# Half-width Fourier stages, with the mirrored half written in reverse, in a hybrid Fourier and attention backbone

## The chip, the cores and the metric

One core of one Trainium2 chip. The metric is the device time of one execution in microseconds. Before the change three runs took 1893.22 to 1894.74 us, median 1894.34.

## What is computed

Two layers over 256 latent tokens and 256 context tokens of width 1024. In each layer a projection feeds two mixers side by side, attention and a two-dimensional Fourier transform of 4 groups of 128 channels; their outputs are gated, merged, projected and added back, and a feed-forward part follows (dense in layer 0, eight experts with two per token in layer 1). The part that matters here:

```python
def fourier_mix(u):
    b, t, _ = u.shape
    ug = u.astype(jnp.float32).reshape(b, t, N_FOURIER_GROUPS, FOURIER_GROUP)
    f = jnp.fft.fft2(ug, axes=(1, 3), norm="ortho").real
    return f.reshape(b, t, FOURIER_WIDTH).astype(u.dtype)
```

Only the real part is kept. With A = u times the channel cosines, B = u times the channel sines, the result is cos(token) A - sin(token) B.

## The kernel before, in words

Activations lie with channels on the 128 partitions and tokens along the free dimension. Weights stream in from HBM through the SP queue, 1 MB at a time; ACT copies each piece to a reduced float32 form (`wh`, L169) and DVE subtracts to get the remainder (`wl`, L181), and a product is taken as three matmuls (`mm3`, L212 to L214). Large activations are held the same way, as a high and a low part.

Within a mixer the order of the instructions is the order in which the Python program writes them. There are two background queues, attention and modulation. Every call of `tick()` gives each queue some credit, and when the credit reaches one, the next step of that queue is written into the program at that place. So pieces of attention (scores L494 to L499, maximum L501 and L503 on DVE, exponentials L512 and L513 on ACT, normalisation L520 to L522 on DVE, transposes L534 on PE, their high part L535 on ACT and low part L536 on DVE, values L546 and `half` L551, L554) stand between the products of the projections, and modulation (L318, L320 on DVE) as well. Each engine then works through its own instructions strictly in that order.

The Fourier part works by group g of 128 channels and by stream s of 256 tokens. Layer 0 has two streams, latent and context; layer 1 has the latent one alone. That makes 8 streams in layer 0 and 4 in layer 1.

- `fourier_first` (L589): for each half of 128 tokens, one float32 matmul of U against `four_c`, 256 columns: 128 cosines, then 128 sines. The two halves share a PSUM tile `psab`; one ACT copy (L598) brings its 512 columns to SBUF as `ab`.
- `fourier_second` (L603): four float32 matmuls of 256 columns (L607, L608) add up the cosine and the sine part over both token halves in one PSUM tile `psf`; ACT copies it to the high part of `ft` (L611), DVE subtracts to get the low part (L612).
- `mixer` (L902) calls them: `first(0)`, the projection of U for group 2, then for g = 0, 1, 2 in layer 0 `second(g)`, `first(g + 1)`, in layer 1 the other way about, and at last `second(3)`. Right behind it `halves(ft)` multiplies all four chunks of `ft` with the weights.

`psab`, `psf` and the projection tiles `psp` share the PSUM tag "mm" with three buffers. The SBUF tag "rr" with two buffers holds the rotary temporaries and `half` of the attention.

Of the kernel before, what the change touches and what calls it, by code (L numbers as in the profile page):

```python
# [11 lines left out]
F32 = mybir.dt.float32  # L12
F32R = mybir.dt.float32r
I32 = mybir.dt.int32
AF = mybir.ActivationFunctionType
OP = mybir.AluOpType
# [5 lines left out]
TL = 256  # L22
# [53 lines left out]
def hybrid_kernel(ctx, tc, x, c, ctx_in, c_ctx, w_mod, b_mod, norm1_g, norm2_g, w_in, sink, w_fourier,  # L76
# [3 lines left out]
    V, A, P_, G, S = nc.vector, nc.scalar, nc.tensor, nc.gpsimd, nc.sync  # L80
# [29 lines left out]
    def tick(n=1):  # L110
        for _ in range(n):
            ticks[0] += 1
            for q in ("attn", "mod"):
                credit[q] += pace[q]
                if credit[q] >= 1.0:
                    credit[q] -= 1.0
                    step(q)
# [470 lines left out]

    def fourier_first(streams, sb, ps_pool, u, nab):  # L589

        r = []
        for s in range(streams):
            ps = ps_pool.tile([128, 2, 256], F32, name="psab", tag="mm", bufs=3)
            for k in range(2):
                t0 = s * 256 + k * 128
                P_.matmul(ps[:, k, :], u[:, t0:t0 + 128], four_c, start=True, stop=True)
            ab = sb.tile([128, 2, 256], F32, name="ab", tag="ab", bufs=nab)
            A.activation(ab, ps, AF.Copy)  # L598
            r.append(ab)
            tick()  # L600
        return r

    def fourier_second(abs_, g, ps_pool, f_out):  # L603
        for s, ab in enumerate(abs_):
            ps = ps_pool.tile([128, 512], F32, name="psf", tag="mm", bufs=3)[:, :256]
            for k in range(2):
                P_.matmul(ps, ab[:, k, 0:128], four_t(0, k), start=(k == 0), stop=False)  # L607
                P_.matmul(ps, ab[:, k, 128:256], four_t(1, k), start=False, stop=(k == 1))  # L608
                tick()
            sl = slice(s * 256, (s + 1) * 256)  # L610
            A.activation(f_out[:, 0, g, sl], ps, AF.Copy)  # L611
            V.tensor_tensor(f_out[:, 1, g, sl], ps, f_out[:, 0, g, sl].bitcast(F32), op=OP.subtract)  # L612

    def mixer_units(l):
        base = l * D * IN_W
# [34 lines left out]
    four_c = tabp.tile([128, 256], F32, name="four_c")  # L650
# [11 lines left out]
    four_t = lambda a, k: tab[1 + a][:, k * 256:(k + 1) * 256]  # L662
# [13 lines left out]
    psA = psA_st.enter_context(tc.tile_pool(name="psA", bufs=2, space=PSUM))  # L676
# [225 lines left out]
    def mixer(l, limbs, r16, psk, psv, when_mixed=None, when_merging=None, pre=(), xp=None, room=None):  # L902
        n = T2 if l == 0 else TL
# [11 lines left out]
        at = attn_st.enter_context(tc.tile_pool(name=f"attn{l}", bufs=1))  # L915
# [33 lines left out]
        U, AB = {}, {}  # L949
# [30 lines left out]
        ft = r16.tile([128, 2, 4, n], F32R, name="ft", tag="ro")  # L980
        o = r16.tile([128, 2, 4, n], F32R, name="o", tag="ro")
# [4 lines left out]
            AB[g] = fourier_first(n // 256, lp, psA, U.pop(g), 2)  # L986

        def second(g):
            fourier_second(AB.pop(g), g, psA, ft)

        def late_q(j):
            while prog["scores"] < 2 * (j - 1) * (n // 128):
# [37 lines left out]
        for p in range(2):  # L1030
            for i, ps in halves(ft):
                f = 4 * p + i
                pool, tag, bufs = ((lp, "U", 2), (lp, "ab", 2), (tabp, "tab", 3), (lp, "q1", 1))[
                    2 * p + (i % 2 if p == 0 else i == 3)]
# [8 lines left out]
            for i in range(4):  # L1043
                f = 4 * p + i
                t = gate(lp, "q0", 1)
# [18 lines left out]
        for p in range(2):  # L1064
            th = early_th[4 * p:4 * p + 4] or [gate(mg, "th", 4) for _ in range(4)]
            for i, ps in halves(o):
                f = 4 * p + i
                y = th[i][:, :n]
                V.scalar_tensor_tensor(y, y, 1.0, ps[:, :n], op0=OP.add, op1=OP.mult)
                if owed:  # L1070
# [4 lines left out]
                                                             op=OP.subtract))  # L1075
# [53 lines left out]
    with ExitStack() as st:  # L1129
# [44 lines left out]
        for a, b in PARTS:  # L1174
            ah = r16.tile([128, 8, T2], F32R, name="ah", tag="ro")
            al = r16.tile([128, 8, T2], F32R, name="al", tag="ro")
            for j in range(a, b, 2):
                sg = []
                for br in range(2):
                    for k in range(2):  # L1180
                        if j == 0 and br == 0:
                            ps = first[k]
                        else:
                            wh, wl = stream.take()
                            ps = psA.tile([128, 512], F32, name="psp", tag="mm", bufs=3)
                            mm3(stream, ps, wh, wl, range(8), [(hh[:, i, :], hl[:, i, :]) for i in range(8)])
                        if br == 0:
                            t = ff.tile([128, 512], F32, name="sg", tag="sg", bufs=3)
                            A.activation(t, ps, AF.Silu)
                            sg.append(t)  # L1190
                        else:
                            i = j - a + k
                            t = ff.tile([128, 512], F32, name="af", tag="af", bufs=2)
# [823 lines left out]
```

## Time and profile before

| | before |
|---|---|
| median of 3 runs, us | 1894.34 |
| profiled execution, us | 1891.14 |
| its span, us | 1889.3 |
| mean granted TensorE clock | 0.991 |
| PE busy, us (share of the span) | 1805.1 (96%) |
| DVE busy, us | 1507.3 (80%) |
| ACT busy, us | 1131.6 (60%) |

The span runs from the first to the last recorded instruction; 1.84 us of the profiled execution lie around it. Busy time is the time in which an engine had at least one instruction at work. The busy times are means over stages with different limits, so windows and the order of instructions in time have to be read beside them. In the rows below, a number in square brackets behind an instruction is the engine's idle time before it, with the engine, tile and line that ended it. PE is the matmul, PEld its weight load.

### The profile page before, as it was taken

The page shows a single profiled execution, that of the slowest core. Times are in us where ns is not written, and L with a number is a line of the kernel's source. Part 1 is how long each engine was busy: PE and PEld are TensorE (multiplying, and loading weights), DVE is VectorE, ACT ScalarE, POOL GpSimd, SP SyncE. Part 2 cuts the span into 40 slices and gives each one's busy share as a digit, 9 for nine tenths or more (in the row PEclk, how much of TensorE's full clock was granted, in tenths as well). Part 3 has the DMA queues.
Part 4 walks back from the last instruction along what each step waited for, and adds up shares of the span by engine and source line. Part 5 has one row for each costly group of instructions (what it writes and reads, how often), then busy time and mean ns, then how long its engine had stood idle before and what let it go on. Part 6 is the DMA issues. An engine that isn't in the chain of part 4 may idle for free. (4 is left out here: it accounts for less than half of the span.)

```text
span 1889.3 us, 27557 instructions
## 1 busy us (share of the span) xinstructions
PE 1805.1 (96%) x9701; PEld 1497.7 (79%) x9701; DVE 1507.3 (80%) x1772; ACT 1131.6 (60%) x1280; POOL 64.2 (3%) x95
## 2 busy tenths in 40 slices
PE   7999999999999999999999999999999999999996
PEld 4788877877777788899877878778887788888874
DVE  6787896577777436787788988999889988888897
ACT  5564622423122223665497877887778887787785
POOL 3200000200000001100000000000000000000000
PEclk9999999999999999999999999999999999999999
DMA  9313462265577223434898999999999999999992
GB/s 295 105 57 101 129 206 91 92 214 196 176 232 261 92 79 100 135 112 157 312 367 321 403 367 363 408 402 408 344 342 408 401 391 333 326 363 371 378 402 104
DMA packets 222530, 488.59 MB, mean 259 GB/s; under 512 B 11410, under 2 KB 106898, under 8 KB 222356
## 3 DMA queue, kind: packets, MB, share of 16 engines
q1 hardware_dynamic: 221076, 482.11, 70.6%
q0 software_dynamic: 1280, 4.20, 0.8%
q8 instruction: 105, 1.72, 0.4%
q14 instruction: 69, 0.57, 0.1%
HBM read 485.22 MB, written 1.05 MB: 257 GB/s over the span
## 5 line engine op out<-in xcount | busy, mean ns | idle before, releaser
L1373 DVE TENSOR_TENSOR el<-raw,eh 128x2048 fp32r<-128x2048 f32 (+2 forms) x333 | 727.7, 2211 | 92.1 <-PE pgt L1830 34.2
L1350 ACT ACTIVATE eh<-raw 128x2048 fp32r<-128x2048 f32 (+2 forms) x333 | 609.6, 1859 | 94.7 <-PE pgt L1830 56.9
L212 PE MATMUL psp<-hh,wh 128*128 128x512 f32 (+1 forms) x704 | 260.1, 370 | 2.6 <-ACT U L954 1.8
L214 PE MATMUL psp<-hh,wl 128*128 128x512 f32 (+1 forms) x704 | 255.6, 363 | 4.9 <-DVE wl L181 4.9
L213 PE MATMUL psp<-hl,wh 128*128 128x512 f32 (+1 forms) x704 | 254.5, 362 | 0.0
L181 DVE TENSOR_TENSOR wl<-raw,wh 128x1024 fp32r<-128x1024 f32 (+1 forms) x152 | 182.4, 1207 | 41.8 <-PE psp L214 20.8
L169 ACT ACTIVATE wh<-raw 128x1024 fp32r<-128x1024 f32 (+1 forms) x152 | 156.3, 1039 | 62.1 <-DMA raw<-in_w_down_d 24.9
L212 PEld LDWEIGHTS psp<-hh,wh 128*128 128x128 f32 x704 | 133.5, 190 | 31.1 <-issue 9.9
L214 PEld LDWEIGHTS psp<-hh,wl 128*128 128x128 f32 x704 | 133.2, 189 | 27.7 <-DVE wl L181 7.4
L213 PEld LDWEIGHTS psp<-hl,wh 128*128 128x128 f32 x704 | 133.5, 190 | 19.4 <-issue 0.5
L1830 PE MATMUL py<-el,eah 128*128 128x256 f32 (+1 forms) x712 | 126.1, 315 | 8.1 <-DVE el L1373 7.1
L1830 PEld LDWEIGHTS py<-el,eah 128*128 128x128 f32 x712 | 102.6, 190 | 35.8 <-DVE el L1373 27.5
L1830 PE MATMUL py<-eh,eah 128*128 128x512 f32 x440 | 121.2, 397 | 0.0
L320 DVE SCALAR_TENSOR_TENSOR acc<-rawm,cvec,acc 128x512 f32<-128x512 f32 x140 | 99.8, 748 | 1.4
L1830 PE MATMUL pup<-el,xh 128*128 128x256 f32 (+1 forms) x560 | 94.7, 307 | 4.4 <-DVE el L1373 4.3
L1830 PEld LDWEIGHTS pup<-el,xh 128*128 128x128 f32 x560 | 80.5, 188 | 20.1 <-DVE el L1373 11.9
L1830 PE MATMUL pgt<-el,xh 128*128 128x256 f32 (+1 forms) x480 | 84.6, 314 | 11.5 <-DVE el L1373 10.9
L1830 PE MATMUL pup<-eh,xh 128*128 128x512 f32 x336 | 93.9, 401 | 0.0
L1830 PEld LDWEIGHTS pgt<-el,xh 128*128 128x128 f32 x480 | 69.4, 189 | 28.5 <-DVE el L1373 20.7
L1830 PEld LDWEIGHTS py<-eh,eah 128*128 128x128 f32 x440 | 78.9, 189 | 14.6 <-ACT eh L1350 0.8
L1830 PE MATMUL pgt<-eh,xh 128*128 128x512 f32 x296 | 83.5, 404 | 0.7 <-ACT xh L1461 0.7
L1195 ACT ACTIVATE ah<-af 128x512 fp32r<-128x512 f32 x22 | 13.9, 632 | 99.7 <-DVE af L1194 99.7
(379 smaller groups left out, 3221.0 us busy)
## 6 DMA issues: line engine op xcount, KB each, us to landing
raw<-in_w_gate_e SPq DMA_DIRECT2D x112, 1024.0 KB, 7.8
raw<-in_w_down_e SPq DMA_DIRECT2D x110, 1024.0 KB, 7.7
raw<-in_w_up_e SPq DMA_DIRECT2D x109, 1024.0 KB, 8.0
rawm<-in_w_mod SPq DMA_DIRECT2D x112, 256.0 KB, 4.5
raw<-in_w_in SPq DMA_DIRECT2D x26, 1024.0 KB, 5.3
raw<-in_w_gate_d SPq DMA_DIRECT2D x11, 1024.0 KB, 5.5
raw<-in_w_up_d SPq DMA_DIRECT2D x11, 1024.0 KB, 5.5
mraw<-in_w_mod SPq DMA_DIRECT2D x16, 512.0 KB, 8.7
```

The source lines that it names most:

```text
L169: A.activation(h[:, :n, :], src, AF.Copy)
L181: self.eng.tensor_tensor(lo[:, :n, :], src, h[:, :n, :].bitcast(F32), op=OP.subtract)
L212: P_.matmul(ps, wh[:, k, :], ah, start=(start and i == 0), stop=False)
L213: P_.matmul(ps, wh[:, k, :], al, start=False, stop=False)
L214: P_.matmul(ps, wl[:, k, :], ah, start=False, stop=(stop and i == n - 1))
L320: V.scalar_tensor_tensor(acc[v], r, s, acc[v], op0=OP.mult, op1=OP.add)
L1195: A.activation(ah[:, i, :], t, AF.Copy)
L1350: A.activation(self.like(self.hi[i][:, sl], x), x, AF.Copy)
L1373: V.tensor_tensor(self.like(self.lo[i][:, sl], x), x, self.like(self.hi[i][:, sl], x).bitcast(F32), op=OP.subtract)
L1830: P_.matmul(ps[:, a:b], x[:, k, :], w[:, c + a:c + b], start=(start and ps_id[i] not in seen), stop=(stop and ps_id[i] not in ps_id[i + 1: ...
```

## The change

`fourier_first` multiplies the channel columns 0 to 64 of the cosines and of the sines alone, 130 columns in place of 256. `fourier_second` multiplies the token columns 0 to 128, 129 in place of 256, and keeps the cosine part (`even`) and the sine part (`odd`) in separate columns of the PSUM tile. The rest follows from cos(2 pi (n - j) k / n) = cos(2 pi j k / n) and the opposite sign for the sine: the missing half of `ab` is written backwards by two more ACT copies, one with scale -1, and the missing half of the result is even minus odd, written backwards by DVE. The sum and the difference form a new SBUF tile `f`, from which the high and the low part of `ft` are made. The temporaries `odd` and `f` take the tag "rr". The number of ticks stays the same.

```diff
     def fourier_first(streams, sb, ps_pool, u, nab):
-        r = []
+        r, h = [], 65
+        two = four_c.rearrange("p (a n) -> p a n", a=2)[:, :, 0:h]
+        turned = lambda t, a: bass.AP(tensor=t.tensor, offset=t.offset + a * 128 + 127,
+                                      ap=[list(t.ap[0]), [256, 2], [-1, 128 - h]])
         for s in range(streams):
-            ps = ps_pool.tile([128, 2, 256], F32, name="psab", tag="mm", bufs=3)
+            ps = ps_pool.tile([128, 2, 2, h], F32, name="psab", tag="mm", bufs=3)
             for k in range(2):
                 t0 = s * 256 + k * 128
-                P_.matmul(ps[:, k, :], u[:, t0:t0 + 128], four_c, start=True, stop=True)
+                P_.matmul(ps[:, k], u[:, t0:t0 + 128], two, start=True, stop=True)
             ab = sb.tile([128, 2, 256], F32, name="ab", tag="ab", bufs=nab)
-            A.activation(ab, ps, AF.Copy)
+            A.activation(ab.rearrange("p k (a n) -> p k a n", a=2)[:, :, :, 0:h], ps, AF.Copy)
+            A.activation(turned(ab, 0), ps[:, :, 0, 1:128 - h + 1], AF.Copy)
+            A.activation(turned(ab, 1), ps[:, :, 1, 1:128 - h + 1], AF.Copy, scale=-1.0)
             r.append(ab)
             tick()
         return r
 
-    def fourier_second(abs_, g, ps_pool, f_out):
+    def fourier_second(abs_, g, ps_pool, f_out, sb):
+        h = TL // 2 + 1
         for s, ab in enumerate(abs_):
-            ps = ps_pool.tile([128, 512], F32, name="psf", tag="mm", bufs=3)[:, :256]
-            for k in range(2):
-                P_.matmul(ps, ab[:, k, 0:128], four_t(0, k), start=(k == 0), stop=False)
-                P_.matmul(ps, ab[:, k, 128:256], four_t(1, k), start=False, stop=(k == 1))
+            ps = ps_pool.tile([128, 512], F32, name="psf", tag="mm", bufs=3)
+            even, odd = ps[:, 0:h], ps[:, 256:256 + h]
+            for i, p in enumerate((even, odd)):
+                for k in range(2):
+                    P_.matmul(p, ab[:, k, i * 128:(i + 1) * 128], four_t(i, k)[:, 0:h], start=(k == 0), stop=(k == 1))
                 tick()
+            o = sb.tile([128, 256], F32, name="odd", tag="rr", bufs=2)
+            f = sb.tile([128, 256], F32, name="f32", tag="rr", bufs=2)
+            A.activation(o[:, 0:h], odd, AF.Copy)
+            V.tensor_tensor(f[:, 0:h], even, o[:, 0:h], op=OP.add)
+            back_ = bass.AP(tensor=f.tensor, offset=f.offset + TL - 1, ap=[list(f.ap[0]), [-1, TL - h]])
+            V.tensor_tensor(back_, even[:, 1:TL - h + 1], o[:, 1:TL - h + 1], op=OP.subtract)
             sl = slice(s * 256, (s + 1) * 256)
-            A.activation(f_out[:, 0, g, sl], ps, AF.Copy)
-            V.tensor_tensor(f_out[:, 1, g, sl], ps, f_out[:, 0, g, sl].bitcast(F32), op=OP.subtract)
+            A.activation(f_out[:, 0, g, sl], f, AF.Copy)
+            V.tensor_tensor(f_out[:, 1, g, sl], f, f_out[:, 0, g, sl].bitcast(F32), op=OP.subtract)
```

In the changed kernel the two matmul lines are L600 and L617, ACT's copies L602, L603, L604 (`ab`), L621 (`odd`) and L626 (`ft`), and DVE's operations L622 (add), L624 (subtract) and L627 (low part of `ft`).

The order on DVE in layer 0, at `second(0)` (its two streams), before; `ft` is the Fourier result, `xlo` the low part of the attention weights, `st` and `p` its softmax:

```order
L503 TENSOR_SCALAR st<-st,sink_b 128x1
L612 TENSOR_TENSOR ft<-psf,ft 128x256
L536 TENSOR_TENSOR xlo<-ptr,xh 128x4x128
L520 TENSOR_TENSOR st<-st 128x1
L521 RECIPROCAL st<-st 128x1
L522 TENSOR_SCALAR p<-p,st 128x512
L612 TENSOR_TENSOR ft<-psf,ft 128x256
L501 TENSOR_REDUCE st<-pss 128x1
```

and in the changed kernel:

```order
L503 TENSOR_SCALAR st<-st,sink_b 128x1
L622 TENSOR_TENSOR f_924<-psf,odd 128x129
L624 TENSOR_TENSOR f_924<-psf,odd 128x127
L627 TENSOR_TENSOR ft<-f_924,ft 128x256
L536 TENSOR_TENSOR xlo<-ptr,xh 128x4x128
L520 TENSOR_TENSOR st<-st 128x1
L521 RECIPROCAL st<-st 128x1
L522 TENSOR_SCALAR p<-p,st 128x512
L622 TENSOR_TENSOR f_949<-psf,odd 128x129
L624 TENSOR_TENSOR f_949<-psf,odd 128x127
L627 TENSOR_TENSOR ft<-f_949,ft 128x256
L501 TENSOR_REDUCE st<-pss 128x1
```

Each place of L612 now holds three instructions in a row, and the attention steps between them stand where they stood.

The order on ACT at the same place, from the second stream of `second(0)` to the end of `first(1)`, before:

```order
L535 ACTIVATE xh<-ptr 128x4x128
L611 ACTIVATE ft<-psf 128x256
L598 ACTIVATE ab<-psab 128x512 x2
L512 ACTIVATE p,st<-pss,st 128x256
L513 ACTIVATE st<-sink_b,st 128x1
```

and in the changed kernel:

```order
L535 ACTIVATE xh<-ptr 128x4x128
L621 ACTIVATE odd<-psf 128x129
L626 ACTIVATE ft<-f_949 128x256
L602 ACTIVATE ab<-psab 128x4x65
L603 ACTIVATE ab<-psab 128x2x63
L604 ACTIVATE ab<-psab 128x2x63
L602 ACTIVATE ab<-psab 128x4x65
L603 ACTIVATE ab<-psab 128x2x63
L604 ACTIVATE ab<-psab 128x2x63
L512 ACTIVATE p,st<-pss,st 128x256
L513 ACTIVATE st<-sink_b,st 128x1
```

The copy of `odd` has come in ahead of the copy to `ft`, which now reads `f`, and each copy of `ab` has become three.

## Rows read from the trace of the kernel before

**Rows 1.** The profile's page, busy us (share of the span) and instructions of each engine.

```profile
PE 1805.1 (96%) x9701; PEld 1497.7 (79%) x9701; DVE 1507.3 (80%) x1772; ACT 1131.6 (60%) x1280; POOL 64.2 (3%) x95
```

**Rows 2.** Windows: length, busy us PE, PEld, DVE, ACT, POOL, then PEclk, DMA, GB/s.

```profile
94.40:130.84 36.44, 36.22 (x199) 31.57 (x198) 31.57 (x87) 22.02 (x62) 2.76 (x5) 1.00 0.23 66
...
130.84:142.30 11.46, 11.46 (x70) 9.96 (x69) 9.82 (x26) 7.88 (x20) 0.54 (x1) 1.00 0.08 23
142.30:151.00 8.70, 8.70 (x40) 7.21 (x39) 2.51 (x6) 2.61 (x6) 0.54 (x1) 1.00 0.48 151
85.30:89.10 3.80, 3.80 (x10) 3.02 (x11) 3.06 (x6) 1.68 (x3) 1.02 (x2) 0.56 0.49 114
779.15:796.98 17.83, 17.83 (x108) 16.32 (x106) 12.18 (x27) 12.27 (x26) 0.00 (x0) 1.00 0.47 147
```

**Rows 3.** Instructions by tile (psab, psf): records, ns min/median/max, first and last start.

```profile
L596 PE MATMUL psab<-four_c,U x48: 377/379/382, 81.1 to 792.7; 128*128 128x256 f32 x48
...
L607 PE MATMUL psf<-tab,ab x48: 377/379/483, 94.2 to 796.3; 128*128 128x256 f32 x48
```

**Rows 4.** Timeline of PE: start us, length us of the merged group, count.

```profile
97.04 0.59 PE L608 MATMUL psf<-tab,ab 128*128 128x256 f32 x2
97.47 0.59 PE L607 MATMUL psf<-tab,ab 128*128 128x256 f32 x2
...
137.75 1.25 PE L292 MATMUL psm<-ones,mx 128*128 128x1 f32 x10
```

**Rows 5.** ACT by line and shape, 60 to 240 us: count, busy us, mean ns, idle before.

```profile
L598 ACT ACTIVATE ab<-psab 128x512 f32<-128x512 f32 x8 | 4.6, 598 | 1.6 <-PE psab L596 1.6
L611 ACT ACTIVATE ft<-psf 128x256 fp32r<-128x256 f32 x8 | 3.1, 382 | 0.8 <-PE psf L608 0.7
L558 ACT ACTIVATE o<-o 128x512 fp32r<-128x512 f32 x4 | 2.5, 632 | 3.9 <-DVE o L554 3.9
```

**Rows 6.** DVE by line and shape, 60 to 240 us, the same columns.

```profile
L554 DVE TENSOR_TENSOR o<-po,half 64x128 f32<-64x128 f32 x32 | 9.0, 282 | 8.4 <-ACT half L551 8.2
...
L612 DVE TENSOR_TENSOR ft<-psf,ft 128x256 fp32r<-128x256 f32 x8 | 3.3, 417 | 0.0
```

**Rows 7.** Timelines of DVE and ACT: two handovers, DVE to ACT and ACT to DVE.

```profile
81.88 0.43 DVE L929 TENSOR_TENSOR q<-rraw,rsh 128x256 f32<-128x256 f32 x1
82.40 1.28 ACT L942 ACTIVATE qs<-q 64x512 fp32r<-64x512 f32 x2 [1.56 <-DVE q L929]
...
132.62 0.63 ACT L558 ACTIVATE o<-o 128x512 fp32r<-128x512 f32 x1 [0.92 <-DVE o L554]
133.28 0.69 DVE L559 TENSOR_TENSOR o<-o,o 128x512 fp32r<-128x512 f32 x1 [0.70 <-ACT o L558]
```

**Rows 8.** Waits of DVE, 94.40 to 130.84: us in total, times, longest us.

```profile
DVE o L554 <- ACT half L551: 2.7, 3, 1.2
DVE st L501 <- PE pss L499: 1.2, 4, 0.4
```

**Rows 9.** Timelines of DVE and PE in layer 0: a wait, last `ft`, its first reader.

```profile
107.78 0.58 DVE L554 TENSOR_TENSOR o<-po,half 64x128 f32<-64x128 f32 x2 [0.35 <-ACT half L551]
130.42 0.41 DVE L612 TENSOR_TENSOR ft<-psf,ft 128x256 fp32r<-128x256 f32 x1
...
132.01 0.39 PE L213 MATMUL psp<-ft,wh 128*128 128x512 f32 x1
```

**Rows 10.** Timeline of PE behind `first(0)` of layer 0.

```profile
85.30 0.50 PE L212 MATMUL psp<-hh,wh 128*128 128x512 f32 x1 [1.78 <-ACT U L954]
```

**Rows 11.** Timelines of ACT, DVE and PE in layer 1: the chain's start and end.

```profile
788.93 0.69 ACT L512 ACTIVATE p<-pss,st 128x512 f32<-128x512 f32 x1
...
797.18 0.38 ACT L611 ACTIVATE ft<-psf 128x256 fp32r<-128x256 f32 x1 [0.49 <-PE psf L608]
797.60 0.42 DVE L612 TENSOR_TENSOR ft<-psf,ft 128x256 fp32r<-128x256 f32 x1 [0.52 <-ACT ft L611]
798.74 0.28 PE L213 MATMUL psp<-ft,wh 128*128 128x256 f32 x1
```

More of the change, by code (lines that the diff above doesn't have):

```diff
@@ L988, in second @@
         def second(g):
-            fourier_second(AB.pop(g), g, psA, ft)
+            fourier_second(AB.pop(g), g, psA, ft, at)
         def late_q(j):
```

## The prediction

> **What bounds the kernel now.** I read the busy table first, then windows cut around the Fourier work, then the order of the instructions there on each engine. The busy table has PE occupied for 1805.1 us of 1889.3 and DVE for 1507.3 [rows 1]. That is an average, so the stages decide. The eight layer-0 streams of the second stage lie at 94.4 to 130.84 us: PE is busy 36.22 of 36.44 us, DVE 31.57, ACT 22.02. In layer 1 the two stages lie at 779.15 to 796.98: PE 17.83 of 17.83, DVE 12.18, ACT 12.27 [rows 2]. So PE sets the pace in both places, and nothing after them breaks the link: PE has no idle time from 130.84 to 151.00 either [rows 2]. What PE gains or loses here moves the end. But in layer 0 DVE is a close second: it has only 36.44 - 31.57 = 4.87 us free.
>
> **PE: what is taken away.** The tile view counts 48 records each for L596 and L607 (L608 is the twin of L607) [rows 3]. A float32 matmul makes two records, so these are 24 first-stage matmuls and 48 second-stage ones, 72 in all. From one pair of records to the next takes 97.47 - 97.04 = 0.43 us [rows 4]; that is one 256-column matmul. The new ones have 130 and 129 columns. No row has that width. The lower end is the L292 group, float32 with one column: ten records in 1.25 us, the last lasting 0.25, so (1.25 - 0.25) / 9 = 0.111 us a record, 0.222 a matmul, which is what its weight loads allow [rows 4]. The upper end is no saving, 0.43. Half of 0.43 is 0.215, under the floor, so I take 0.222: a saving of 0.21 us each, 72 x 0.21 = **15.1 us** of PE time. Of it 44 matmuls (12 first, 32 second) lie in the layer-0 window, 9.2 us; 24 lie in the layer-1 window, 5.0 us; the four of layer 0's `first(0)` come earlier.
>
> **ACT: what is added.** A 512-column copy from PSUM takes 598 ns, a 256-column one 382 [rows 5]: 0.84 ns a column over a fixed 0.166 us. So the main copy of `ab`, 260 columns, is about 0.39 us and each turned copy of 126 about 0.27. Neighbours overlap by some 0.1 us, hence 0.74 us in place of 0.60, +0.14 a stream. The copy of the odd half, 129 columns, is 0.275; nearest rows below and above give 0.17 (the fixed part) and 0.382. The last copy, 256 columns, now reads SBUF: at 512 columns SBUF costs 632 against 598 ns [rows 5], so 0.42. No row writes with a step of -1. I take it at the price of a forward write, the nearest row there is; as the upper end I allow twice that, +0.27 us for each turned piece.
>
> **DVE: what is added.** An addition and a subtraction of 129 and 127 columns. The nearest row is L554, 128 columns from PSUM and SBUF: 282 ns [rows 6], back to back 0.29 apart, so 0.58 for the two (upper end 2 x 0.417, the 256-column L612 [rows 6]). The last subtraction keeps its size.
>
> **The path, not the sums.** Before, one ACT copy and one DVE subtraction followed each other once. Now the work bounces: ACT copies odd, DVE adds and subtracts, ACT copies the sum, DVE subtracts. DVE takes its instructions in order, and between its second and third operation nothing else stands in its queue. So it waits there for ACT: handover to ACT 82.40 - (81.88 + 0.43) = 0.09 us, the copy 0.42, handover back 133.28 - (132.62 + 0.63) = 0.03 [rows 7]. A stream therefore holds DVE for 0.58 + 0.09 + 0.42 + 0.03 = **1.12 us** longer. Behind it on DVE stand the softmax steps of the attention and the low halves that PE's transposes and projections wait for; PSUM tiles of the "mm" tag, three of them, also come free only with DVE's subtraction, so PE cannot run far ahead.
>
> Eight streams in layer 0: 8 x 1.12 = **9.0 us** on DVE. Against it stand its waits on PE, which disappear when PE is early: 1.2 us in this window [rows 8], 0.95 without the one at its start, and the first wait for `half`, 0.35 us [rows 9]. The later waits for `half` stay, since ACT's copy of it now also stands behind a copy that waits for DVE. So DVE ends the last low half of `ft` 9.0 - 1.3 = 7.7 us late. It ended at 130.42 + 0.41 = 130.83 before; PE used it at 132.01 [rows 9]. The 1.18 us between are a cushion: PE is **6.5 us late** at the first product that reads the last group. All 9.2 us saved on PE turn into waiting. From there PE was and is the bound [rows 2]; DVE is busy only 2.51 of 8.70 us at 142.30 to 151.00, where it makes up its extra 1.2 us. PE's lateness stays.
>
> `first(0)` of layer 0 gains nothing: right behind it PE sat idle for 1.78 us until ACT had copied U [rows 10]. It finishes 0.84 us sooner and waits 0.84 us longer.
>
> Layer 1 is a chain on ACT. From the copy behind the table load at 788.93 [rows 11] I add up, with overlaps, in the new order: 0.3 us late to begin with (the bounce of group 0 stands ahead of the table load); softmax 0.86, weight split 0.95, U 0.26, `ab` 0.63, softmax 0.85, bounce of group 1 with 0.275 + 0.03 + 0.58 + 0.09 + 0.32 = 1.30, `ab` 0.63, bounce of group 2 1.30, softmax 0.85, and the last bounce to the end of its copy 1.40. That is 9.03 us, so 788.93 + 0.3 + 9.03 = 798.3, and the low half 0.45 later, 798.7. Before, copy and low half were done at 797.56 and 798.02, and PE used the low half at 798.74 [rows 11]. So PE is where it was: **0 us**. Its 5.0 us become waiting as well.
>
> **Sum:** 0 + 6.5 + 0 = +6.5 us. Against the profiled execution, 1891.14 us (span 1889.3 and 1.84 around it), that is 1897.6. The median of the runs shown is 1894.34, 3.2 us above the profiled one; on that scale I predict **1901 us**.
>
> **Rivals.** *Faster: the bounce is hidden.* If ACT's last copy overlaps DVE work after all, DVE pays only the two operations, 8 x 0.58 = 4.6 us, which fits in its free 4.87 us [rows 2]: layer 0 comes out even, and layer 1, where DVE is idle for 5.65 of 17.83 us, keeps its 5.0 us: 1894.3 - 5.0 = 1889.3. It decides once a stream costs DVE less than 4.87 / 8 = 0.61 us. For it: the two margins are small sums. Against it: the copy's input is made by the DVE instruction just ahead, and its reader is the next one. Even with DVE free of charge, layer 0 could not gain more than 4.87 us; the full 15 us are out of reach. The Trainium skill speaks for this rival in part (VectorE: DVE Perf Modes, "The DRAIN you can't avoid"): instructions on DVE pay for their number, while a semaphore between them adds nothing. By that rule the sum would be 4.6 us on DVE; the measured case there has one engine, and the rows here show 0.09 and 0.03 us for a handover between two, with the copy itself in between [rows 7]. 20%.
>
> *Half.* Some of the waiting falls together with waits that were there (for `half`, for `o`), or layer 1 gains 2 or 3 us and layer 0 loses as much: about 1895, no change. 18%.
>
> *Slower by the clock.* After the 1.78 us of idle time, PE ran at a granted clock of 0.56 over 85.30 to 89.10, mostly the lower level of 1.2 GHz [rows 2, 10]; half speed over 3.8 us cost about 1.7 us. The change makes several such gaps. Where PE has time to spare this is free, but behind the last one in each layer it is not, and a slower second stage also feeds the bounce later: 2 to 3 times 1.7, 1904.5 to 1906. 12%.
>
> *It does not do what it says.* Were a narrow float32 matmul priced like a wide one, PE would save nothing; both engines would be late, and the result lies with the slower ones. The weight-load row speaks against it.
>
> **Chances.** Forecast 50%, faster rival 20%, half 18%, clock 12%. A measurement of this kernel tells about 0.2%, 3.8 us, from no change. So faster 20%, the same 18%, slower 62%. The range starts just under the faster rival, 1888, and ends at 1908: clock rival plus the turned copies at up to twice their price.
>
> **What would show it.** Right: records of L600 and L617 at about 0.11 us; DVE idle ahead of L627 for about 0.5 us in each of the 12 streams, waiting for ACT; ACT idle ahead of L626, waiting for DVE; PE idle 14 to 17 us in layer 0 between the first psf and the first product from `ft`, waiting for ACT's `ab`, for DVE and for `ft`; the third chunk's product near 138.5 instead of 132.0; a granted clock under 1 in that stretch. Wrong: PE idle less than 9 us there, or L626 starting without a wait, or layer 1 ending its second stage 3 us or more early.

## The result and the profile after

| | before | after |
|---|---|---|
| median of the runs compared | 1892.88 (1891.04 to 1894.74) | 1902.15 (1899.74 to 1904.52) |
| ratio, 95% interval | | 1.0053 [1.0043, 1.0063] |
| profiled execution | 1891.14 | 1901.58 |
| its span, mean granted clock | 1889.3, 0.991 | 1899.9, 0.985 |

The change made the kernel slower by half a per cent, 9.3 us between the medians. The median before is of six runs, three more than the 1894.34 us above rests on. The busy line of the page, which answers to [rows 1]:

```profile
PE 1800.7 (95%) x9701; PEld 1494.9 (79%) x9701; DVE 1511.8 (80%) x1796; ACT 1135.5 (60%) x1316; POOL 64.2 (3%) x95
```

PE has less work and DVE 24 more instructions, two in each of the 12 streams. The sums on this line hardly move; the Fourier stretch does. Windows of the changed kernel, columns as in [rows 2]; the first is the former window, the second reaches from its first `psf` product to its first product with `ft`:

```profile
94.40:130.84 36.44, 26.50 (x158) 23.32 (x157) 27.69 (x81) 20.05 (x69) 1.61 (x3) 0.85 0.18 53
91.89:132.95 41.06, 31.12 (x190) 27.94 (x189) 31.98 (x92) 22.43 (x74) 2.76 (x5) 0.84 0.19 54
```

PE was busy 36.22 us of this window before and is busy 26.50 now. No engine is full any more: DVE 27.69, ACT 20.05. What bounds a stretch in which all engines idle is a chain that goes from one to the next. The tile views of `psab`, `psf` and `ft` give the durations and the chain (count, ns minimum/median/maximum, first and last start):

```profile
L600 PE MATMUL psab<-four_c,U x48: 272/273/378, 79.2 to 802.1; 128*128 128x130 f32 x48
L602 ACT ACTIVATE ab<-psab x12: 372/386/416, 83.3 to 804.1; 128x260 f32<-128x260 f32 x12
L603 ACT ACTIVATE ab<-psab x12: 265/272/309, 83.5 to 804.4; 128x126 f32<-128x126 f32 x12
L604 ACT ACTIVATE ab<-psab x12: 277/286/325, 83.7 to 804.6; 128x126 f32<-128x126 f32 x12
...
L617 PE MATMUL psf<-tab,ab x96: 271/275/583, 91.9 to 805.6; 128*128 128x129 f32 x96
L621 ACT ACTIVATE odd<-psf x12: 265/278/314, 94.5 to 807.1; 128x129 f32<-128x129 f32 x12
L622 DVE TENSOR_TENSOR f<-psf,odd x12: 282/285/293, 96.1 to 807.5; 128x129 f32<-128x129 f32 x12
L624 DVE TENSOR_TENSOR f<-psf,odd x12: 279/279/291, 96.3 to 807.7; 128x127 f32<-128x127 f32 x12
...
L626 ACT ACTIVATE ft<-f x12: 416/416/418, 96.6 to 808.1; 128x256 fp32r<-128x256 f32 x12
L627 DVE TENSOR_TENSOR ft<-f,ft x12: 424/425/426, 97.1 to 808.5; 128x256 fp32r<-128x256 f32 x12
```

Below the durations, the view of `ft` says what an engine waited for (first line) and who waited (second line), in us and times:

```profile
  DVE f L624: 15.3, 12
...
  DVE ft L627: 5.8, 12
```

ACT waited 12 times for DVE's difference ahead of its copy L626, 15.3 us in all, and DVE waited 12 times for that copy ahead of L627, 5.8 / 12 = 0.48 us each. PE's waits from 70 to 320 us (us in total, times, longest) show where this arrives; before, PE waited 1.8 us for U, 2.0 us for a transpose's input and 0.2 us for `ab` here, no more:

```profile
PE psf L617 <- ACT ab L603: 5.5, 2, 4.9
...
PE psp L212 <- DVE f L624: 1.6, 1, 1.6
PE psab L600 <- DVE f L624: 1.5, 2, 1.1
PE psf L617 <- DVE ft L627: 1.4, 1, 1.4
...
PE psp L212 <- ACT ft L626: 0.5, 1, 0.5
```

The longest wait, 4.9 us, is only in part the handover's: 1.52 us of it are ACT's wait for DVE, the rest ACT's copies and attention work ahead of them; with the copy issued earlier (an experiment below) PE waits 2.97 us at this place. It can be followed through three timelines (start, length, in brackets the idle time just before and who ended it). DVE:

```profile
118.12 0.28 DVE L622 TENSOR_TENSOR f<-psf,odd 128x129 f32<-128x129 f32 x1
118.32 0.28 DVE L624 TENSOR_TENSOR f<-psf,odd 128x127 f32<-128x127 f32 x1
119.08 0.43 DVE L627 TENSOR_TENSOR ft<-f,ft 128x256 fp32r<-128x256 f32 x1 [0.48 <-ACT ft L626]
...
121.88 0.69 DVE L501 TENSOR_REDUCE st<-pss 128x1 f32<-128x512 f32 x1 [1.58 <-PE pss L499]
```

ACT and PE in the same place:

```profile
116.83 0.28 ACT L621 ACTIVATE odd<-psf 128x129 f32<-128x129 f32 x1
118.63 0.42 ACT L626 ACTIVATE ft<-f 128x256 fp32r<-128x256 f32 x1 [1.52 <-DVE f L624]
118.96 0.37 ACT L602 ACTIVATE ab<-psab 128x260 f32<-128x260 f32 x1
119.22 0.27 ACT L603 ACTIVATE ab<-psab 128x126 f32<-128x126 f32 x1
...
119.54 1.23 PE L617 MATMUL psf<-tab,ab 128*128 128x129 f32 x4 [4.90 <-ACT ab L603]
```

ACT had copied the odd half and then stood 1.52 us until DVE got round to the sums. The copies of `ab`, whose input was ready, stand behind it in ACT's queue. PE needs them for the next `psf`, and the scores of the attention stand behind that `psf` in PE's queue; so DVE, for which ACT had stood, then waits 1.58 us for those scores. The end of the stretch, first DVE's last low half of layer 0, then PE's first product that reads it, which answer to 130.42 and 132.01 in [rows 9]:

```profile
137.04 0.42 DVE L627 TENSOR_TENSOR ft<-f,ft 128x256 fp32r<-128x256 f32 x1 [0.48 <-ACT ft L626]
...
137.52 0.50 PE L213 MATMUL psp<-ft,wh 128*128 128x512 f32 x1
```

For a ledger I took three instructions that every kernel here has: the second group of L292 on PE (modulation, behind layer 0's Fourier stretch), the first L379 of layer 1's normalisation, and the last product with `o` in layer 1, behind its Fourier stretch. Their starts, all from profiled executions:

| kernel | L292 | L379 | last with `o` | median of runs | ratio to before, 95% interval |
|---|---|---|---|---|---|
| before | 195.03 | 744.93 | 900.61 | | |
| after | 201.65 | 751.69 | 910.93 | 1902.15 | 1.0053 [1.0043, 1.0063] |
| first stage only | 194.90 | 744.88 | 899.10 | 1889.61 | 0.9988 [0.9978, 0.9997] |
| second stage only | 202.41 | 752.30 | 910.37 | 1902.94 | 1.0053 [1.0040, 1.0066] |
| full-width matmuls | 202.56 | 752.72 | 909.95 | 1903.80 | 1.0067 [1.0054, 1.0080] |
| high half from PSUM | 203.06 | 752.78 | 911.83 | 1902.89 | 1.0060 [1.0047, 1.0073] |
| the same, issued earlier | 197.03 | 747.28 | 904.10 | 1893.27 | 0.9993 [0.9983, 1.0003] |
| no sums | 195.89 | 745.91 | 901.92 | 1909.88 | 1.0085 [1.0069, 1.0100] |
| second stage in layer 1 only | 194.43 | 744.32 | 902.47 | 1891.61 | 0.9991 [0.9982, 1.0001] |
| split one stream later | 195.54 | 745.68 | 902.67 | 1894.28 | 1.0008 [0.9998, 1.0018] |
| sums on GpSimd | 194.87 | 747.50 | 902.56 | 1894.07 | 1.0009 [1.0000, 1.0018] |
| low half there too | 197.35 | 747.55 | 902.10 | 1892.30 | 0.9999 [0.9990, 1.0008] |

Of the 10.4 us between the two profiled executions, 6.6 are there at L292 and do not change for 550 us (6.8 at L379). Some 3.5 more arise between L379 and the last product with `o`; behind that the two run level.

The three columns of starts are of one execution each, and these do not start level. The first product of `first(0)`, ahead of which all kernels are the same, starts at 81.06 before, at 79.19 in the changed kernel and between 79.53 and 80.67 in the others. So differences of up to 2 us between two kernels in the column of L292 say little. Counted from that product, L292 is later than before by 8.5 us in the changed kernel, 0.8 with the first stage alone, 2.8 in "the same, issued earlier" and 1.5 with the split one stream later.

### The profile page after: what moved, and what is told of

The parts are those of the page before. It is cut to its first block, busy times and chain, and to the rows that moved or that the text cites. A ratio compares the mean times of both kernels' runs of the same rounds, so it can differ in the third digit from the quotient of the medians.

```text
span 1899.9 us, 27626 instructions
## 1 busy us (share of the span) xinstructions
PE 1800.7 (95%) x9701; PEld 1494.9 (79%) x9701; DVE 1511.8 (80%) x1796; ACT 1135.5 (60%) x1316; POOL 64.2 (3%) x95
```

## The experiments

The first theory is the prediction's: each stream of the second stage holds DVE for its two sums (0.56 us by the medians above) and for the handover to ACT and back (0.48). The rivals were PE's narrow matmuls, the reversed copies of the first stage, the sums alone, and TensorE's granted clock.

**First stage only.** The first stage of the change with the second stage of before.

```
-            even, odd = ps[:, 0:h], ps[:, 256:256 + h]
-            for i, p in enumerate((even, odd)):
...
+                P_.matmul(ps, ab[:, k, 0:128], four_t(0, k), start=(k == 0), stop=False)
+                P_.matmul(ps, ab[:, k, 128:256], four_t(1, k), start=False, stop=(k == 1))
...
-            A.activation(f_out[:, 0, g, sl], f, AF.Copy)
-            V.tensor_tensor(f_out[:, 1, g, sl], f, f_out[:, 0, g, sl].bitcast(F32), op=OP.subtract)
+            A.activation(f_out[:, 0, g, sl], ps, AF.Copy)
+            V.tensor_tensor(f_out[:, 1, g, sl], ps, f_out[:, 0, g, sl].bitcast(F32), op=OP.subtract)
```

> Only the first stage is changed; the second is that of before. The first theory (the bounce: DVE waits for ACT's copy between its operations in the second stage, and does two operations more, which makes DVE the bound of layer 0) expects no loss: DVE has not one instruction more, ACT 0.14 us more a stream, and PE saves 20 x 0.21 = 4.2 us where it was the bound. So 1 to 5 us faster than before, about 1889. A rival, that the backward copies on ACT are what costs (three copies in place of one, each ahead of the second stage's matmuls), expects a good part of the 9.3 us lost here: 1896 or more.

1889.61 us, 0.03 to 0.22% faster than before: the reversed copies of `ab` cost nothing that ends on the path. The gain is not in layer 0 (-0.1 us at L292) but in layer 1: -1.5 at the last product with `o` (0.8 of it between the first and the last masked score behind 780 us), where eight matmuls at the predicted saving of 0.21 us would give 1.7.

**Second stage only.** The other way round: `fourier_first` as before, `fourier_second` as changed.

```
-                P_.matmul(ps[:, k], u[:, t0:t0 + 128], two, start=True, stop=True)
+                P_.matmul(ps[:, k, :], u[:, t0:t0 + 128], four_c, start=True, stop=True)
...
-            A.activation(turned(ab, 0), ps[:, :, 0, 1:128 - h + 1], AF.Copy)
-            A.activation(turned(ab, 1), ps[:, :, 1, 1:128 - h + 1], AF.Copy, scale=-1.0)
...
+            A.activation(ab, ps, AF.Copy)
```

> Only the second stage is changed; the first is that of before. The first theory expects the whole loss of the change, or a little more, since the first stage's saving is gone: 8 to 12 us slower than before, ratio 1.004 to 1.0065, with DVE idle for 0.48 us ahead of the last subtraction in all 12 streams. The rival with the backward copies on ACT expects about half of it or less, under 5 us.

1902.94 us, the time of the whole change. All of the loss is in the second stage.

**Full-width matmuls.** The change with 256 columns in both stages again, copies and sums left as they are.

```
-                P_.matmul(ps[:, k], u[:, t0:t0 + 128], two, start=True, stop=True)
+                P_.matmul(ps[:, k].rearrange("p a n -> p (a n)"), u[:, t0:t0 + 128], four_c, start=True, stop=True)
...
-                    P_.matmul(p, ab[:, k, i * 128:(i + 1) * 128], four_t(i, k)[:, 0:h], start=(k == 0), stop=(k == 1))
+                    P_.matmul(p, ab[:, k, i * 128:(i + 1) * 128], four_t(i, k), start=(k == 0), stop=(k == 1))
```

> The changed kernel, but both stages multiply all columns again (256 in each matmul); the copies and the additions take the first half of them, as in the change, so only PE gets its 15.1 us back. The first theory expects nearly the time of the change, since what PE saved became waiting: 0 to 4 us above it, 9 to 13 us above before. If PE's work still set the pace, the time would rise by the whole 15.1 us, to 24 above before. A third theory, that the loss is mostly TensorE's granted clock (0.82 to 0.84 over 40 us in the profile of the change) dropped by its idle gaps, expects fewer gaps, a clock of 0.95 or more from 100 to 140 us, and a time below the change by 3 us or more.

1903.80 us. The 15.1 us of PE's work that the change takes away are worth 1.7 us between the medians, and the two intervals overlap, so it may be nothing. The third theory falls as well. The granted clock was 1.00 in every window from 100 to 140 us, two of which are shown, where it was 0.82 to 0.84 in the changed kernel, and the time is no better:

```profile
110.00:120.00 10.00, 6.64 (x37) 5.68 (x36) 7.62 (x23) 4.88 (x18) 0.54 (x1) 1.00 0.41 121
120.00:130.00 10.00, 9.77 (x52) 8.43 (x51) 6.77 (x20) 5.94 (x23) 0.00 (x0) 1.00 0.06 21
```

**High half from PSUM.** To take DVE's wait away, ACT's copy to `ft` reads the even part in `psf`, written twice over the 256 places, and DVE subtracts that from the sums: `ft` still adds up to the sums, split at another point.

```
-            A.activation(f_out[:, 0, g, sl], f, AF.Copy)
+            A.activation(f_out[:, 0, g, sl].rearrange("p (r n) -> p r n", r=2),
+                         ps[:, None, 0:128].to_broadcast([128, 2, 128]), AF.Copy)
```

> The changed kernel, but ACT's last copy (256 columns, the high part of ft) reads the even half in PSUM twice over instead of the sum that DVE makes, so it waits for PE alone; DVE's last subtraction takes the rest, f minus this high part, into the low part. Same number and size of instructions in the same order. What is left out is the exact split: the low part is now as large as the high part and rounded, so the output is less exact. The wait of ACT for DVE and of DVE for ACT is gone, the two extra DVE operations stay. The first theory expects most of the loss gone: 8 streams x 0.5 = 4 us less on DVE in layer 0, and layer 1's chain shorter by 4 x 1 us: between 4 us faster and 3 us slower than before. If the work on DVE and ACT alone made the loss, without the waiting, the time stays that of the change, 7 us or more above before.

A miss: 1902.89 us, as the change. But the waits that it should have removed are still in its tile view of `ft`:

```profile
L626 ACT ACTIVATE ft<-psf x12: 383/383/386, 98.2 to 809.0; 128x256 fp32r<-128x256 f32 x12
...
  DVE f L624: 15.2, 12
...
  DVE ft L628: 5.4, 12
```

ACT no longer needs what DVE makes, and waits for it all the same, 15.2 us in 12 places, because both read `psf` and the copy is written behind the difference. The edit changed the data and not the wait, so it said nothing about the wait's price. The Trainium skill has a rule for this (PSUM — Partial Sum Buffer, "PSUM bank collisions raise a hardware error"): the compiler's scheduler adds a dependency between any two instructions on different engines that touch the same bank in the same quadrant of 32 partitions, two reads included. The row, 15.2 us in 12 waits between two reads of `psf`, agrees with it; what put this wait in is not shown by any run.

**The same, issued earlier.** The same copy, now written ahead of the two sums (`twice` is the even part as above).

```
             A.activation(o[:, 0:h], odd, AF.Copy)
+            A.activation(f_out[:, 0, g, sl].rearrange("p (r n) -> p r n", r=2), twice, AF.Copy)
             V.tensor_tensor(f[:, 0:h], even, o[:, 0:h], op=OP.add)
             V.tensor_tensor(back_, even[:, 1:TL - h + 1], o[:, 1:TL - h + 1], op=OP.subtract)
-            A.activation(f_out[:, 0, g, sl].rearrange("p (r n) -> p r n", r=2), twice, AF.Copy)
             V.tensor_tensor(f_out[:, 1, g, sl], f, f_out[:, 0, g, sl].bitcast(F32), op=OP.subtract)
```

> As in the run without a handover, the high half is taken from the even part in PSUM, written twice over the 256 places, and the low half is the sums less that; so ft's numbers are others. New is the order: the high copy is issued right behind the odd copy and ahead of the two sums, because in the earlier run ScalarE still waited for the second sum ahead of each of the 12 high copies (15.2 us in all) and VectorE still waited 0.45 us ahead of each low half. Theory 1 (VectorE's order is late by what it waits and works in each stream, 0.48 + 0.58 us): the 0.48 us goes 8 times in layer 0, 3.9 us, and ScalarE's copies of ab no longer stand behind that wait: 1895 to 1899 us. Theory 2 (the two sums alone are the cost, or the narrow matmuls, not the handover): 1901 to 1904 us, with VectorE's idle time ahead of the low half gone all the same.

1893.27 us, lower than the first theory's range (1895 to 1899) and no longer to be told from before. One instruction moved up by two places in the program. On ACT and on DVE the order of the instructions is what it was in the run before, the high copy reads the same data, the medians of the durations differ by 9 ns at most, and `odd` and `f` still share the tag "rr"; so neither the narrow matmuls nor the shared buffers are needed to explain the loss. DVE and ACT at the place shown above (timelines):

```profile
117.07 0.28 DVE L625 TENSOR_TENSOR f<-psf,odd 128x129 f32<-128x129 f32 x1
117.27 0.28 DVE L627 TENSOR_TENSOR f<-psf,odd 128x127 f32<-128x127 f32 x1
117.58 0.43 DVE L628 TENSOR_TENSOR ft<-f,ft 128x256 fp32r<-128x256 f32 x1
...
115.78 0.28 ACT L623 ACTIVATE odd<-psf 128x129 f32<-128x129 f32 x1
115.95 0.38 ACT L624 ACTIVATE ft<-psf 128x256 fp32r<-128x256 f32 x1
116.22 0.40 ACT L602 ACTIVATE ab<-psab 128x260 f32<-128x260 f32 x1
```

No wait on either engine, and the copies of `ab` begin at 116.22 where they began at 118.96. At L292 the lateness falls from 8.0 us (203.06, the run before) to 2.0. The 6.0 us (5.6 counted from `first(0)`) are more than DVE's own wait. From 70 to 150 us DVE waited 3.6 us for the high copy, 3.3 for `half` and 2.5 for the scores in the run before, and 0, 2.1 and 1.6 us here: 3.6 us are the wait itself, and 2.1 came off the waits for what stood behind it on ACT and PE. The 2.0 that are left are no price of the sums: without any sums 0.9 are left (next run), and with all of them, split later, 0.5.

**No sums.** Odd copy and sums left out; high and low half are both taken from the even part written twice. The stage's result is thus another, and so is all that follows from it.

```
-            A.activation(o[:, 0:h], odd, AF.Copy)
-            V.tensor_tensor(f[:, 0:h], even, o[:, 0:h], op=OP.add)
-            V.tensor_tensor(back_, even[:, 1:TL - h + 1], o[:, 1:TL - h + 1], op=OP.subtract)
...
-            A.activation(f_out[:, 0, g, sl], f, AF.Copy)
+            A.activation(f_out[:, 0, g, sl].rearrange("p (r n) -> p r n", r=2), twice, AF.Copy)
```

> The recombination is left out: no odd copy, no sums; high and low half are taken from the even part in PSUM, written twice over the 256 places. Narrow matmuls and the reversed first stage stay as the change has them, and so does the pair of instructions per stream that the kernel before had (one ScalarE copy of 256 places, one VectorE subtraction of 256). Theory 1 (the loss is what the recombination puts on VectorE and between the engines): the time of the kernel with the first stage alone, or up to 3 us less, 1886 to 1891 us. Rival (the narrow matmuls, the tile with its two halves, or a change of phase against the rest cost the time): 1897 us or more.

1909.88 us, slower than everything: a miss of the first theory's 1886 to 1891 and inside the rival's range, but no verdict on the stage. Up to L292 the kernel is nearly level with before (+0.9). The loss lies behind the last product with `o`: from there to the end of the span it is 1912.1 - 901.9 = 1010 us, against 1889.3 - 900.6 = 989 before. The page shows why the two can't be compared:

```profile
PE 1832.5 (96%) x9689; PEld 1522.0 (80%) x9689; DVE 1512.1 (79%) x1773; ACT 1136.1 (59%) x1305; POOL 64.6 (3%) x95
```

9689 matmuls, 9701 in all the others: the experts take one of two ways by the number of tokens routed to them, and other numbers in `ft` route other tokens.

**Second stage in layer 1 only.** Layer 0 has the second stage of before, layer 1 the changed one.

```
-            fourier_second(AB.pop(g), g, psA, ft, at)
+            if l:
+                fourier_second(AB.pop(g), g, psA, ft, at)
+            else:
+                fourier_full(AB.pop(g), g, psA, ft)
```

> The changed second stage only in the second of the two layers, the former one in the first layer; the reversed first stage in both. Theory 1 (the whole loss arises in the first layer's Fourier stretch, and the slow clock behind 755 us in the profiles of the change follows from arriving there some 7 us later): 1888 to 1892 us, granted clock 1.00 between 750 and 770 us. Rival (each layer's stage costs its part, or the clock falls there whatever happened before): 1894 us or more.

1891.61 us: the loss arises in layer 0, as far as the interval can tell; some 1.3 us of layer 1, which its profile shows, would not stand out. The other half of the expectation fell. The clock did drop between 750 and 770 us, though this kernel arrived there 0.6 us earlier than before; see the last section.

**Split one stream later.** The whole change, with high and low half of a stream issued behind the next stream's sums or `ab` copies. The temporaries `odd` and `f` also get tags of their own in place of "rr".

```
-            A.activation(f_out[:, 0, g, sl], f, AF.Copy)
-            V.tensor_tensor(f_out[:, 1, g, sl], f, f_out[:, 0, g, sl].bitcast(F32), op=OP.subtract)
...
+            later_.append(split)
+            if len(later_) > 1:
+                later_.pop(0)()
```

> The whole change, but each stream's split into high and low half is issued one stream later (behind the next stream's sums, or behind the next stream's copies of the first stage), with tiles of their own for the odd part and the sums; the last one is issued at once. Nothing is left out. Theory 1: the two waits of 0.48 us and the waits of ScalarE for the sums go, the 0.58 us of sums per stream stays, so the lateness at the end is some 8 x 0.58 = 4.6 us less the 1.2 us cushion, and part of the clock's loss: 1894 to 1899 us. Rival (VectorE's work alone is the cost): 1900 to 1903 us; rival (a split that stands later holds up the product): above 1903 us.

1894.28 us, at the low end of the first theory's range. It computes everything the change computes, and layer 0 is 0.5 us late instead of 6.6. So DVE can carry the sums almost free in layer 0, if nobody stands and waits for them. Against the first stage alone the kernel is still 0.2% slower, and the two intervals do not touch. In the profiled executions 3.6 us lie between the two at the last product with `o`, 0.6 of them ahead of L292 and most behind L379, where the granted clock fell to 0.56 in the one (755 to 760 us) and kept 1.00 in the other; whether that holds for the other runs is not shown.

**Sums on GpSimd, and the low half there too.** Both are built on the split one stream later. ACT copies both halves of `psf` in one instruction, GpSimd makes difference and sum; in the second kernel it makes the low half as well, but for the last stream of a layer.

```
-            V.tensor_tensor(f[:, 0:h], even, o[:, 0:h], op=OP.add)
+            G.tensor_tensor(f[:, 0:h], f[:, 0:h], o, op=OP.add)
...
+                low = V if g == 3 and s == len(abs_) - 1 else G
```

> As the run with the split one stream later, and besides the sum and the difference are made by GpSimd: ScalarE copies both halves of psf in one instruction to SBUF, GpSimd writes the difference in reverse and then the sum, and VectorE keeps only the low half, as in the kernel before. Nothing is left out. Theory 1 (what is left of the loss is the 0.58 us of sums per stream on VectorE, whose order sets the first layer's end): the first layer ends as with the first stage alone, 1889 to 1892 us, and below the run with the split later by 1 to 4 us. Rival (GpSimd's two operations are slow enough that ScalarE's high copy waits for them and holds the copies of ab and the softmax behind it): 1895 us or more, with ScalarE idle ahead of the high copies for GpSimd.

> As the run with the sums on GpSimd, and GpSimd makes the low half too, in all streams but the last of each layer; VectorE has no work in the second stage then, 0.42 us less per stream than in the kernel before. Nothing is left out. Theory 1 (VectorE's order sets the end of the first layer's Fourier stretch): 7 x 0.42 = 2.9 us come off in the first layer, 1886 to 1890 us. Rival (the softmax's chain over three engines sets it, not VectorE's sum of work): the time of the run with the sums on GpSimd, 1889 to 1893 us. Rival (GpSimd's low halves come too late for the first products with ft): 1894 us or more, with TensorE idle ahead of a product for GpSimd.

1894.07 and 1892.30 us. Layer 0 behaves as the first theory says for the first of them: L292 starts at 194.87, the first stage alone gave 194.90. The time does not follow: both miss the first theory's range (1889 to 1892, 1886 to 1890). The second lies in that of its first rival, that not DVE's sum of work sets the end of layer 0. In the profiled execution of the first 2.7 us went between L292 and L379, where the code is that of before and the granted clock was 0.83 from 380 to 390; ACT waited 2.4 us in 4 places for GpSimd's sums. The second has its loss ahead of L292, where the clock was 0.87 and 0.78 from 130 to 150. The operations themselves, from the tile views of the second kernel:

```profile
L628 POOL TENSOR_TENSOR f<-f x12: 446/458/935, 95.6 to 799.0; 128x127 f32<-128x127 f32 x12
L629 POOL TENSOR_TENSOR f<-f x12: 457/461/876, 96.6 to 799.5; 128x129 f32<-128x129 f32 x12
...
L635 POOL TENSOR_TENSOR ft<-f,ft x10: 720/730/907, 99.8 to 800.0; 128x256 fp32r<-128x256 f32 x10
L635 DVE TENSOR_TENSOR ft<-f,ft x2: 477/477/477, 129.5 to 800.5; 128x256 fp32r<-128x256 f32 x2
```

None of the kernels with the whole change gets below before by more than its interval. The best kernel is the first stage alone, 1889.61 us.

## Why the prediction held, step by step

The forecast was 1901 us, slower because of the handover between ACT and DVE; it came out at 1902.15. That the two are so near is luck in part: as a difference the sum was +6.5 us, and +9.3 were measured between the medians (+10.4 between the profiled executions), but the forecast started from a median of 1894.34 that six runs put at 1892.88. The mechanism was right: the handover holds DVE, and PE's saving turns into waiting. Layer 0's term came out near its size because the errors of its pieces offset each other; layer 1's was put at nothing and measured 1.3 us.

- *PE, 72 matmuls, 15.1 us.* The pitch held: eight L617 records from 93.45 on take 1.06 us in PE's timeline, the last of them 0.27, so (1.06 - 0.27) / 7 = 0.113 us a record against 0.111. Nearly all of it became waiting, as the run at full width shows.
- *ACT's prices.* 386, 272, 286, 278 and 416 ns against 0.39, 0.27, 0.27, 0.275 and 0.42. A step of -1 costs a copy nothing: L603 writes 126 columns in reverse at the price of the fit through forward copies. On DVE the reversed difference (279 ns) costs what the forward sum costs (285).
- *DVE, 1.12 us a stream.* Measured from the start of L622 to that of L627: 119.08 - 118.12 = 0.96 us. The two sums start 0.20 apart where I had put 0.29, and the handover to ACT takes 0.03 instead of 0.09. The wait stands ahead of all 12 L627, and L626 waits for DVE 12 times.
- *7.7 us late, 6.5 behind the cushion.* DVE ended its last low half at 137.46 instead of 130.83, 6.6 late; PE's reader came at 137.52, with 0.06 us left of the 1.18 us cushion, 5.5 late, and L292 is 6.6 late. The size is right, by pieces that offset each other. DVE's extra is 8 x 0.96 = 7.7 us and not 9.0. Its waits for `half` and for the scores were to shrink by 1.3 us; they grew by 1.2, from 3.9 to 5.1, with one of 1.58 us over ACT's queue and the scores. In return PE began the stretch 2.3 us sooner, its first `psf` at 91.89 instead of 94.21, and 1.9 of that are a sooner `first(0)` in this execution, no work of the change: 7.7 + 1.2 - 2.3 = 6.6. The product that was put near 138.5 came at 137.52; it reads the fourth chunk, not the third.
- *PE idle 14 to 17 us.* Measured 41.06 - 31.12 = 9.9 us, near the 9 under which I had called the forecast wrong. PE ran at a granted clock of 0.84 there, so the same work took longer. The same stretch before, first `psf` product to first product with `ft`:

```profile
94.21:128.79 34.58, 34.36 (x189) 29.96 (x188) 29.62 (x80) 21.55 (x61) 2.76 (x5) 1.00 0.23 69
```

34.36 less the 9.2 saved is 25.2 us of work, and PE was busy 31.12: some 6.0 us went into the slower clock, by this estimate. The two together, 15.9, make the predicted sum. Where the clock stayed at 1.00 from 100 to 140 us, in the run at full width, L292 is as late (+7.5), so the clock did not cause the lateness.
- *Layer 1, 0 us.* From the first masked score behind 780 us to the last one the changed kernel took 65.56 us, before 64.22; the split one stream later also took 64.22. So the term is off by 1.3 us in this execution, and by the same in the kernel with the changed stage in layer 1 alone (65.52). What failed is the start of the chain and not the chain. ACT's timeline of the changed kernel, which answers to 788.93 and 797.18 in [rows 11]:

```profile
799.45 0.69 ACT L512 ACTIVATE p<-pss,st 128x512 f32<-128x512 f32 x1
...
808.06 0.42 ACT L626 ACTIVATE ft<-f 128x256 fp32r<-128x256 f32 x1 [0.66 <-DVE f L624]
```

From 799.45 to the end of the copy at 808.48 are 9.03 us, to the digit what was added up. But the chain starts 4.41 us behind the first masked score (795.04), and before it was 2.86 us (786.07): it is 1.55 us late at its start, and not the 0.3 put down for the handover of group 0.
- *The clock rival*, 12%, holds a part of the truth: some 2.2 us went between 751.69 and 795.04, where the granted clock fell to 0.50. That it is the change's doing is not shown.
- *The faster rival* was wrong for the change as it is and right about the point from which it decides. It said that without the handover the two operations fit into DVE's free 4.87 us; with the split one stream later layer 0 came out 0.5 us late. Its 5.0 us in layer 1 did not appear in any run.

What stays open: no run had DVE's own wait without the wait in ACT's queue, so the split of the 6.0 us above is an account of DVE's idle time and not an experiment on each part. Of the loss behind L379, the part of the clock is not explained.

## What to carry to other kernels

An instruction's price is its duration only while nobody waits in front of it. When a change sends a value from one engine to another and back, follow what is queued behind the waiting instruction on both, and move the return leg later (or the independent copy earlier) before the arithmetic is blamed: here a shift of two places was worth 9.6 us, and 15 us of saved matmuls were worth 1.7, which may be nothing. An experiment that takes away data must be seen to take away the wait, in its own trace, before its time says anything; and where control flow depends on the numbers, one that changes the numbers can be read only up to that point.

## What the runs showed that was not expected

ACT's read of `psf` waited for DVE's read of the same tile, as told above.

The granted clock falls behind idle time that another execution passes unharmed. Windows of the changed kernel, 755 to 770 us, and of the kernel with the changed stage in layer 1 only, 750 to 760:

```profile
755.00:760.00 5.00, 3.35 (x19) 2.75 (x18) 4.23 (x11) 2.52 (x6) 2.23 (x4) 0.85 0.63 193
760.00:765.00 5.00, 5.00 (x24) 4.96 (x24) 2.42 (x7) 1.24 (x3) 2.63 (x4) 0.50 0.07 20
765.00:770.00 5.00, 4.98 (x37) 4.60 (x35) 4.24 (x12) 3.40 (x6) 3.79 (x5) 0.97 0.00 0
```

```profile
750.00:755.00 5.00, 4.12 (x21) 3.81 (x21) 3.34 (x11) 3.67 (x7) 2.84 (x6) 0.66 0.61 201
755.00:760.00 5.00, 5.00 (x28) 4.81 (x28) 2.63 (x8) 1.43 (x4) 2.32 (x3) 0.65 0.01 3
```

Before, PE made the same three pauses here (0.86, 0.48 and 0.88 us) and kept 1.00 in every window from 745 to 770. 0.50 is the lower level, 1.2 GHz. Eight of the twelve profiled kernels dropped at this place, and before, the first stage alone and both kernels with GpSimd's sums did not. Lateness does not decide it, since the kernel that arrived first dropped. The medians of the runs' mean clock are 0.990 for before, 0.989 for the first stage alone and 0.9855 for the change, but also 0.989 for two kernels that dropped here in their profile. With one profile of each kernel it is not shown that the drop is the change's doing, and what decides it was not settled.

GpSimd took 0.46 us for each sum where DVE took 0.28, and 0.73 for the low half where DVE took 0.43, with single ones up to 0.93. The Trainium skill (GPSIMD Engine Reference, "3. Performance versus the Vector engine") gives 1.96 times the Vector engine's time for a float32 addition of 2048 columns; the rows give 1.6 to 1.7 at 129 and 256 columns here, where DVE's sums read PSUM and GpSimd's read SBUF.
